# Six modulation sums move from VectorE to TensorE, and the weight ring becomes ten fixed blocks of 16 KB

## The chip, the cores and the metric

The kernel runs on one core of a Trainium2 chip. The metric is the device time of one execution in microseconds (us). A core has five instruction streams that matter here: TensorE (PE, the matrix engine, whose weight loads the profile lists apart as PEld), VectorE (DVE), ScalarE (ACT), GpSimd (POOL), and SyncE (SP), which issues all of this kernel's transfers (DMAs) between the main memory (HBM) and the on-chip memory (SBUF, 128 partitions). TensorE writes into PSUM, of which the kernel uses eight banks of 128x512 float32.

## The reference

One block of a network on 256 tokens of width 1024, all in float32: a modulated hybrid mixer and a mixture of experts.

```
mod = silu(c) @ w_ada + b_ada                    # [6 * 1024]
sh1, sc1, ga1, sh2, sc2, ga2 = split(mod, 6)
h = rms_norm(x, nw[0]) * (1 + sc1) + sh1
y = concat(gated_delta_rule(...), chunk_band_attention(...)) @ w_out    # both from h @ w_in
x = x + ga1 * rms_norm(y, nw[1])
h = rms_norm(x, nw[2]) * (1 + sc2) + sh2
top 4 of 32 experts per token from h @ w_router + b_router, softmax over the 4
expert e: hu = h @ w_up[e] + b_up[e]; glu = min(hu[:, :1024], 7); lin = clip(hu[:, 1024:], -7, 7)
          act = glu * sigmoid(1.702 * glu) * (lin + 1);  act @ w_down[e] + b_down[e]
x = x + ga2 * rms_norm(sum of gate * expert, nw[3])
```

The modulation is a product of one vector of 1024 with a matrix of 1024 x 6144, 25 MB. The experts' weights are 32 x 3 x 1024 x 1024 float32, 403 MB, and each of them is read once.

## The kernel before

**Stages.** The *front* computes the modulation, h, the projections, the delta rule (in the code `chain`), attention, the output projection, the second norm and the router. Then come the *experts*, in 14 groups.

**Modulation.** The matrix is cut into 12 chunks of 512 columns. A chunk in SBUF is a block of 128 x 8 x 512: row k * 128 + p of the matrix lies in partition p. Four chunks (sh1 and sc1) are summed first, by TensorE (`colvec`, L191). The eight others, the late chunks, are numbered 0 to 7: `seg` = i // 2 says which vector (0 ga1, 1 sh2, 2 sc2, 3 ga2) and `hf` = i % 2 which half of it. `ADA` (L28) gives the way in which each is summed, in `modrow` (L716):

- "D": VectorE multiplies row block 0 by silu(c) in place (L723) and adds the seven others with one multiply-add each (L725), 128x512 every one; then four matmuls against ones (L728) add over the partitions and put the sums into columns.
- "P": `colvec` does eight matmuls (L196) with silu(c), broadcast over 32 columns, as the stationary operand. Four of them at a time write four strips of 32 partitions of one bank. ScalarE copies the bank (L199), and four matmuls against an indicator (L201) add the strips and put the sums into columns.

After either, VectorE adds the bias and, where needed, the norm's weight (L733, L736). `ADATAG` says into which block a chunk is loaded (wF, or wB for chunks 2 and 7), so the chunks in wF follow one another: a chunk is loaded when the one before it has been read. `ADAPOS` says after which step of the projections, attention and output projection the chunk is written into the program (chunk 0 at 5, 4 at 8, 3 at 12, 6 at 19, 1 and 5 at 31; 2 at 6, 7 at 32).

**Order of work.** The program is written step by step, and then a planner orders each engine's instructions, SP's transfers too, by a simulated timeline, with the written order as priority; the `chain` is written with high priority. From L1043 to L1086 the order of TensorE and VectorE is as written: the second half of the output projection (`wout_a`), the residual, the second norm, the router.

**Splits.** The projections run as three products of rounded float32 (fp32r) pairs: `split` (L205) has ScalarE round a weight half-block of 128x2048 into a tile for the high part, and VectorE and GpSimd subtract it from the block to leave the low part there. The tiles for the high part come in turn from a pool tag "wh" with three buffers of 8 KB per partition; every third split uses the tag "h2" instead (`whx`). "h2", 8 KB, also holds, one after the other, x scaled (`xt`), attention's bias (`strip`) and the output projection's result (`yb`). After the 13 splits that use "wh" its turn stands at the second buffer.

**The ring.** The experts are ordered by load; a group holds 2 experts (P), 4 (Q) or 1 (S) side by side in the 128 rows of a matmul, in the order PQPPSQPPSQPPPP. For each of six weight blocks j (0 to 3 up, 4 and 5 down), a group loads one block of 2 MB per expert into the next places of a ring of ten (L23, `slot`, L1094). Eight places are fixed blocks of 16 KB per partition. The places "wh" and "wx" are made of two pool tiles of 8 KB each (`wslot`, L1098): wh of two buffers of the tag "wh", wx of the third and of "h2". `eload` (L1107) loads the blocks of one j in pieces: two in groups 0 (j = 5 only), 1 and 2, four for the last j of all, and otherwise one, but two for every block of that j when a place of it has two tiles:

```
tss = [wslot(slot()) for _ in regs]
m = 8 // max(pieces, max(len(ts) for ts in tss))
for k in range(0, 8, m):
    for reg, ts in zip(regs, tss):
```

Experts 0 and 1 of the order are loaded without waiting for the router. `group` (L1125) then runs, for each j, the 8 matmuls per expert (L1123, 512 columns), the activation, four transposes per half, and the products with the gates (L1172), which VectorE adds to the result.

Of the kernel before, what the change touches and what calls it, by code (L numbers as in the profile page):

```python
# [8 lines left out]
F32 = mybir.dt.float32  # L9
F32R = mybir.dt.float32r  # L10
# [9 lines left out]
NEG = -1e30  # L20
D = 1024
NE = 32
RINGTAGS = ["wB", "w0", "wC", "wE", "w1", "wD", "wF", "wh", "wA", "wx"]  # L23
PB = {"mm": 3, "dl": 3, "tp": 2}
K2 = 4
K1 = 6
KV = 2
ADA = list("DDPDDPDD")  # L28
ADATAG = list("FFBFFFFB")
ADAPOS = [5, 31, 6, 12, 8, 31, 19, 32]  # L30
ADABANK = "tp"
# [4 lines left out]

SINGLES, QUADS = 2, 3
ORDER = "PQPPSQPPSQPPPP"
WH = 3
RS_N = -2.0 * (-2.0 * (-2.0) ** 3) ** 3  # L40

C_C, C_BADA, C_NORM, C_CONV, C_AB, C_RT = 0, 8, 56, 88, 136, 200
# [7 lines left out]
def block_kernel(ctx, tc, x, small, rows, rel_ext, wpre, wexp, b_up, b_down, out,  # L50
                 dbg=None, stop=None):
    nc = tc.nc
    P = 128
# [5 lines left out]

    base = (nc.sbuf_base + 31) // 32 * 32
    ctx.enter_context(nc.sbuf_tensor("fixed", [P, 8 * 4096], F32))
    fixed = {}
    for i, tag in enumerate(("w0", "w1", "wA", "wB", "wC", "wD", "wE", "wF")):
        fixed[tag] = [nc.alloc_sbuf_tensor_at(f"{tag}_{d_}", (P, 4096), dt, offset=base + 16384 * i).ap()
                      for d_, dt in (("f", F32), ("r", F32R))]

    const = ctx.enter_context(tc.tile_pool(name="const", bufs=1))
    mem = ctx.enter_context(tc.tile_pool(name="mem", bufs=1))  # L70
    ps = ctx.enter_context(tc.tile_pool(name="ps", bufs=1, space=PSUM))

    def bank(tag="mm"):
        return ps.tile([P, 512], F32, tag=tag, bufs=PB[tag], name=tag)

    def block(tag):
        return fixed[tag][0]

    def wload(i, tag):
        t = block(tag)  # L80
        nc.sync.dma_start(t, wpre[i])
        return t.rearrange("p (k n) -> p k n", k=8)
# [86 lines left out]
        V.scalar_tensor_tensor(k2("junk"), srcs[1], 1.0, srcs[1], op0=ALU.mult, op1=ALU.mult, accum_out=pt_[:, 1:2])  # L169
        return pt_  # L170

    xt = mem.tile([P, 2, D], F32, tag="h2", name="xt")
    csil = const.tile([P, 8], F32, name="csil")
    rs1 = [rs_of(sumsq(f"ss1{a}", [x2[:, a, n * 512:n * 512 + 512] for n in range(2)]), D, f"rs1{a}", True)
           for a in range(2)]
# [24 lines left out]
        for m in range(4):  # L200
            T.matmul(out_cols[:, m:m + 1], ev[:, m * 128:(m + 1) * 128], ind, start=True, stop=True)  # L201

    nsp = [0]

    def split(w, kv=None, steps=1, extra=None, copy=None):  # L205


        sr, wl = w
        kv = kv or KV
        wh = extra  # L210
        if wh is None:
            wh = mem.tile([P, 2048], F32, tag="wh", bufs=WH, name="wh").bitcast(F32R)
        kn = sr.shape[1]
        wh = wh.rearrange("p (k n) -> p k n", k=kn)
        st = kn // steps
        for k in range(0, kn, st):
            (copy or S.copy)(wh[:, k:k + st], sr[:, k:k + st])
            m = k + kv // steps
            V.tensor_sub(wl[:, k:m], sr[:, k:m], wh[:, k:m])
            w_ = max(1, 512 // sr.shape[2])  # L220
            for i in range(m, k + st, w_):
                G.tensor_sub(wl[:, i:i + w_], sr[:, i:i + w_], wh[:, i:i + w_])
        return wh, wl
# [113 lines left out]
    V.tensor_copy(wabx[0], sm[:, C_AB:C_AB + 64])  # L337
    V.tensor_sub(wabx[1], sm[:, C_AB:C_AB + 64], wabx[0])
    kqT = mem.tile([P, 4, 2, 256], F32, tag="acc", name="kqT")
    whx = mem.tile([P, 2048], F32R, tag="h2", name="whx")  # L340
    spr = bank("dl")
    ws["q"] = hload(5, "wC")
    ws["qb"] = hload(6, "w0")
# [139 lines left out]
    yb = None  # L483
# [232 lines left out]
    def modrow(seg, hf, w):  # L716

        if ADA[2 * seg + hf] == "P":
            b_ = bank("tp")
# [23 lines left out]
        S.copy(dst[:, hf * 512:hf * 512 + 512], rb)  # L743

    def attention(blS):
        strip = mem.tile([P, 8, 256], F32, tag="h2", name="strip")
        nc.sync.dma_start(strip, bass.AP(tensor=rel_ext.tensor, offset=rel_ext.offset,
                                         ap=[[1, P], [384, 8], [1, 256]]))
        G.tensor_scalar(strip[0:64, :, 0:64], strip[0:64, :, 0:64], NEG, None, op0=ALU.add)
        jobs = [(0, 0), (1, 0), (1, 1)]  # L750
        st = {}

        def scores(a, gi):
            nk = 128 * (a + 1)
            hp = 512 // nk
            bs = [bank(), bank()]
            for i in range(hp):
                for par in range(2):
                    r_ = slice(64 * par, 64 * par + 64)
                    pr_ = gi * hp + i  # L760
                    T.matmul(bs[par][:, i * nk:(i + 1) * nk], qbT[r_, pr_, a * 128:(a + 1) * 128], kbT[r_, pr_, 0:nk],
                             start=True, stop=True)
            for par in range(2):
                h0 = 2 * gi * hp + par
                sc = blS[:, 512 * (2 * (a + gi) + par):512 * (2 * (a + gi) + par) + 512].rearrange("p (h k) -> p h k", h=hp)
                V.tensor_add(sc, bs[par].rearrange("p (h k) -> p h k", h=hp),
                             strip[:, h0:h0 + 2 * hp - 1:2, 0:nk][:, :, ::-1])
                mxs = const.tile([P, hp], F32, tag="mxs", bufs=3, name="mxs")
                V.tensor_reduce(mxs, sc, axis=AX.X, op=ALU.max, negate=True)
                dn = const.tile([P, hp], F32, tag="dens", bufs=3, name="dens")  # L770
                for i in range(hp):
                    S.activation(sc[:, i, :], sc[:, i, :], AF.Exp, bias=mxs[:, i:i + 1], accum_out=dn[:, i:i + 1])
                V.reciprocal(dn, dn)
                G.tensor_mul(sc, sc, dn[:, :, None].to_broadcast([P, hp, nk]))
                st[a, gi, par] = sc

        def trans(a, gi):
            nk = 128 * (a + 1)
            hp = 512 // nk
            for par in range(2):  # L780
                sc = st[a, gi, par]
                tp = bank("tp")
                for z_ in range(4):
                    i, kt = z_ // (a + 1), z_ % (a + 1)
                    T.transpose(tp[:, z_ * 128:(z_ + 1) * 128], sc[:, i, kt * 128:(kt + 1) * 128], ident)
                S.copy(sc.rearrange("p h (k t) -> p (h k t)", t=128), tp)

        def av(a, gi):
            nk = 128 * (a + 1)
            hp = 512 // nk  # L790
            if gi == 0:
                st["av", a] = bank()
            b_ = st["av", a]
            for i in range(hp):
                for kt in range(a + 1):
                    for par in range(2):
                        sc = st[a, gi, par].rearrange("p h (k t) -> p h k t", t=128)
                        pr_ = gi * hp + i
                        hd = 2 * pr_ + par
                        T.matmul(b_[64 * par:64 * par + 64, pr_ * 128:(pr_ + 1) * 128], vb[:, kt, hd * 64:(hd + 1) * 64],  # L800
                                 sc[:, i, kt, :], start=kt == 0, stop=kt == a)
            if gi == (0, 1)[a]:
                dst = oxb[0][:, :, a * 128:(a + 1) * 128]
                bv = b_.rearrange("p (k t) -> p k t", k=4)
                S.copy(dst, bv)
                V.tensor_sub(oxb[1][:, :, a * 128:(a + 1) * 128], bv, dst)

        for f, *at in ((scores, 0, 0), (scores, 1, 0), (trans, 0, 0), (scores, 1, 1), (av, 0, 0), (trans, 1, 0), (av, 1, 0),
                       (trans, 1, 1), (av, 1, 1)):
            f(*at)  # L810
            yield
# [48 lines left out]
        run(st_)  # L860

    pos = steps(mixed(), 17)
    yb = mem.tile([P, 2, D], F32, tag="h2", name="yb")
    wo.append(hload(19, "w1", 4))
    steps(wout_b(), pos)
    spa = [split(blk["wo"][n], kv=KW, extra=(fixed["w0"][1][:, 0:2048] if n == 0 else None)) for n in range(2)]
# [227 lines left out]
    def slot():  # L1094
        rtag[0] += 1
        return RINGTAGS[(rtag[0] - 1) % len(RINGTAGS)]

    def wslot(tag):  # L1098

        if tag in ("wh", "wx"):  # L1100
            ts = [mem.tile([P, 2048], F32, tag="wh", bufs=WH, name="wh") if tag == "wh" or i == 0 else
                  mem.tile([P, 2048], F32, tag="h2", name="wx") for i in range(2)]
        else:
            ts = [block(tag)]
        return [t.rearrange("p (k n) -> p k n", n=512) for t in ts]

    def eload(regs, j, pieces=1):  # L1107

        tss = [wslot(slot()) for _ in regs]
        m = 8 // max(pieces, max(len(ts) for ts in tss))  # L1110
        for k in range(0, 8, m):
            for reg, ts in zip(regs, tss):
                src = wexp[reg * 6 + j] if isinstance(reg, int) else wexp[bass.ds(reg * 6 + j, 1)].rearrange("o p n -> p (o n)")
                kt = 8 // len(ts)
                nc.sync.dma_start(ts[k // kt][:, k % kt:k % kt + m].rearrange("p k n -> p (k n)"), src[:, k * 512:(k + m) * 512])
        return [lambda k, ts=ts: ts[k * len(ts) // 8][:, k % (8 // len(ts)), :] for ts in tss]

    def expert_mm(b_, lhs, ws, last=True):

# [151 lines left out]

    fin = fixed[RINGTAGS[-4]][0].rearrange("p (i a d) -> p i a d", i=2, a=2)
    ss3 = const.tile([P, 4], F32, name="ss3")
# [7 lines left out]
    for gi, grp in enumerate(groups):  # L1281
        regs = [r if r < 2 else nc.sync.value_load(sig[0:1, r:r + 1], min_val=0, max_val=NE - 1) for r in grp]
# [26 lines left out]
    with tc.For_i(0, n_ov):  # L1309
# [14 lines left out]
        reg = nc.sync.value_load(eo[0:1, 0:1], min_val=0, max_val=NE - 1)  # L1324
# [77 lines left out]
```

## Time and profile before

| | us |
|---|---|
| median of 3 runs | 1191.61 |
| lowest and highest | 1190.53, 1195.18 |
| profiled execution, its own time | 1192.22 |
| its span, first to last instruction | 1190.4 |
| TensorE busy | 1029.8 (87%) |
| VectorE busy | 358.7 (30%) |
| ScalarE, GpSimd busy | 190.3 (16%), 104.1 (9%) |
| read from HBM | 449.50 MB, 379 GB/s over the span |

The profile is of one execution. "Busy" is the time in which an engine executes; idle time in brackets stands ahead of an instruction, with what ended it. Matmuls overlap, so a group's time is the union of its records. A float32 matmul leaves two records. The clock column is TensorE's granted clock, as a share of full speed. The names w_f and w_r stand for w0 and w1 together. "x16" is the number of instructions merged into one row; a row has its start, its time, engine, line, operation, and output <- input with shapes. For SP a row is an issue of a transfer, not its run.

### The profile page before, as it was taken

What the parts mean: (1) busy time and instruction counts of PE and PEld (TensorE: products, weight loads), DVE (VectorE), ACT (ScalarE), POOL (GpSimd) and SP (SyncE); (2) the same over time, 40 slices, a digit from 0 to 9 for tenths busy, and PEclk for the clock granted to TensorE, in tenths of its full rate; (3) what the DMA queues carried; (4) which work ended last, traced back from release to release, by engine and by line L of the source; (5) the groups of instructions that cost most, each with busy time, mean ns of one, the idle gap of its engine ahead of it and who ended that gap; (6) DMA issues with size and microseconds to landing.
All of it is one profiled execution on the core that took longest, in us unless ns stands there. A gap on an engine that the chain in (4) does not pass through costs nothing. (4 is left out here: it accounts for less than half of the span.)

```text
span 1190.4 us, 14727 instructions
## 1 busy us (share of the span) xinstructions
PE 1029.8 (87%) x5845; PEld 495.3 (42%) x5845; DVE 358.7 (30%) x851; ACT 190.3 (16%) x380; POOL 104.1 (9%) x91
## 2 busy tenths in 40 slices
PE   4898999899977789999976788989967698998985
PEld 2697998654321224435421233335322142433331
DVE  5387888654103022122111012122201011111113
ACT  3453327331001001011000001011001001010101
POOL 1557514200000000000000000000000000000001
PEclk9899999989998999999997999999988899999998
DMA  9925346989999999999999999999999999999993
GB/s 362 403 81 213 142 178 237 401 353 386 421 421 422 421 408 426 423 428 423 423 422 424 427 425 426 424 427 425 420 426 425 423 427 423 426 426 422 428 419 149
DMA packets 51463, 451.93 MB, mean 380 GB/s; under 512 B 5760, under 2 KB 7424, under 8 KB 9408
## 3 DMA queue, kind: packets, MB, share of 16 engines
q1 hardware_dynamic: 51392, 450.97, 91.3%
q8 instruction: 47, 0.77, 0.3%
q14 instruction: 24, 0.20, 0.0%
HBM read 449.50 MB, written 1.05 MB: 379 GB/s over the span
## 5 line engine op out<-in xcount | busy, mean ns | idle before, releaser
L1123 PE MATMUL dl<-w_f,xg 128*64 128x512 f32 (+1 forms) x224 | 113.5, 653 | 9.7 <-DMA w_f<-in_wexp_dram 9.7
L1177 DVE TENSOR_TENSOR acc<-acc,mm 128x512 f32<-128x512 f32 x52 | 35.8, 688 | 242.2 <-PE mm L1172 242.2
L1123 PE MATMUL mm<-w_f,xg 128*64 128x512 f32 (+2 forms) x208 | 92.7, 594 | 4.0 <-DMA w_f<-in_wexp_dram 4.0
L1279 POOL TENSOR_TENSOR wF_f<-acc,m_row 128x512 f32<-128x512 f32 x3 | 3.8, 1273 | 943.1 <-DMA w_f<-in_wexp_dram 937.3
L1123 PE MATMUL dl<-wh,xg 128*64 128x512 f32 (+2 forms) x144 | 70.3, 633 | 5.1 <-DMA wh<-in_wexp_dram 5.1
L1123 PE MATMUL dl<-wD_f,xg 128*64 128x512 f32 (+1 forms) x128 | 65.4, 662 | 4.3 <-DMA wD_f<-in_wexp_dram 4.3
L1172 PE MATMUL mm<-yg,wts 128*128 128x512 f32 x112 | 54.5, 614 | 11.0 <-ACT yg L1169 10.0
L1141 ACT ACTIVATE sg<-gm 128x512 f32<-128x512 f32 x28 | 17.6, 630 | 288.9 <-DVE gm L1139 263.1
L1123 PE MATMUL dl<-wE_f,xg 128*64 128x512 f32 (+2 forms) x112 | 55.2, 645 | 6.4 <-DMA wE_f<-in_wexp_dram 6.4
L1123 PE MATMUL mm<-wB_f,xg 128*64 128x512 f32 (+2 forms) x128 | 57.6, 595 | 0.0
L1123 PE MATMUL mm<-wh,xg 128*64 128x512 f32 (+1 forms) x144 | 57.1, 594 | 0.5 <-DMA wh<-in_wexp_dram 0.5
L1123 PE MATMUL dl<-wF_f,xg 128*64 128x512 f32 (+2 forms) x112 | 54.5, 628 | 2.8 <-DMA wF_f<-in_wexp_dram 2.8
L1123 PE MATMUL dl<-wC_f,xg 128*64 128x512 f32 (+2 forms) x112 | 55.4, 638 | 1.4 <-DMA wC_f<-in_wexp_dram 1.4
L1003 PEld LDWEIGHTS tp<-oh,x 128*128 128x128 f32 x432 | 50.7, 192 | 13.2 <-issue 11.4
L1003 PE MATMUL tp<-oh,x 128*128 128x128 f32 x432 | 54.8, 279 | 0.7 <-ACT aT__3377 L1152 0.7
L1123 PE MATMUL mm<-wE_f,xg 128*64 128x512 f32 (+1 forms) x112 | 49.6, 595 | 3.9 <-DMA wE_f<-in_wexp_dram 3.9
L1169 ACT COPY yg<-dl 128x512 f32<-128x512 f32 x27 | 15.8, 585 | 224.8 <-PE dl L1123 224.8
L1123 PE MATMUL dl<-wB_f,xg 128*32 128x512 f32 (+1 forms) x96 | 47.7, 634 | 3.5 <-DMA wB_f<-in_wexp_dram 3.5
L1013 DVE TENSOR_SCALAR xg<-tp,mc,mc 128x128 f32<-128x128 f32 x52 | 19.6, 405 | 101.1 <-PE dl L1123 92.4
L1123 PE MATMUL mm<-wC_f,xg 128*64 128x512 f32 (+1 forms) x112 | 50.0, 594 | 0.0
L1123 PEld LDWEIGHTS dl<-w_f,xg 128*64 128x64 f32 (+1 forms) x224 | 28.2, 134 | 42.6 <-issue 25.7
L1139 DVE TENSOR_SCALAR gm<-dl 128x512 f32<-128x512 f32 x14 | 9.7, 692 | 119.5 <-PE dl L1134 119.5
(640 smaller groups left out, 2193.3 us busy)
## 6 DMA issues: line engine op xcount, KB each, us to landing
wh<-in_wexp_dram SPq DMA_DIRECT2D x57, 1024.0 KB, 24.7
w_f<-in_wexp_dram SPq DMA_DIRECT2D x26, 2048.0 KB, 26.1
wA_f<-in_wexp_dram SPq DMA_DIRECT2D x36, 1024.0 KB, 22.2
wF_f<-in_wexp_dram SPq DMA_DIRECT2D x36, 1024.0 KB, 29.7
wE_f<-in_wexp_dram SPq DMA_DIRECT2D x15, 2048.0 KB, 29.4
wC_f<-in_wexp_dram SPq DMA_DIRECT2D x15, 2048.0 KB, 27.0
wB_f<-in_wexp_dram SPq DMA_DIRECT2D x13, 2048.0 KB, 22.2
wD_f<-in_wexp_dram SPq DMA_DIRECT2D x13, 2048.0 KB, 34.2
```

Of the source, the lines that this page charges most:

```text
L1003: T.matmul(b_[:, k * 128:(k + 1) * 128], x2[:, a, half(n)][:, k * 128:(k + 1) * 128], oh[:, a], start=a == tiles[0], stop=a == tiles[-1])
L1013: V.tensor_scalar(xg[:, k], src, mc, sc, op0=ALU.mult, op1=ALU.add)
L1123: T.matmul(b_[i * n:(i + 1) * n, :], lhs[:, k, i * n:(i + 1) * n], w(k), start=k == 0, stop=last and k == 7)
L1139: V.tensor_scalar(gm, bs[0], 7.0, None, op0=ALU.min)
L1141: S.activation(sg, gm, AF.Sigmoid, scale=1.702)
L1169: S.copy(yg, b_)
L1172: T.matmul(cb, wt[:, a], yg, start=True, stop=True)
L1177: V.tensor_add(acc[:, a, sl], acc[:, a, sl], cb)
L1279: (V if a and n else G).tensor_mul(fin[:, 0, a, sl], acc[:, a, sl], m3_row[:, sl])
```

## The change

All eight late chunks are summed in the form "P". The fixed region grows from eight to ten blocks of 16 KB: wG and wH are new. The high parts of the splits now lie, in turn, in the first half of wG, the second half of wG and the first half of wH (`highs`), and what used the tag "h2" lies in the second half of wH (`h2`). The pool tags "wh" and "h2" go, so the memory in use stays the same. In the ring wG and wH stand where wh and wx stood, and `eload` no longer cuts their sets in two.

```diff
-RINGTAGS = ["wB", "w0", "wC", "wE", "w1", "wD", "wF", "wh", "wA", "wx"]
+RINGTAGS = ["wB", "w0", "wC", "wE", "w1", "wD", "wF", "wG", "wA", "wH"]
...
-ADA = list("DDPDDPDD")
+ADA = list("PPPPPPPP")
...
-    ctx.enter_context(nc.sbuf_tensor("fixed", [P, 8 * 4096], F32))
+    ctx.enter_context(nc.sbuf_tensor("fixed", [P, 10 * 4096], F32))
...
+    highs = [fixed["wG"][1][:, 0:2048], fixed["wG"][1][:, 2048:4096], fixed["wH"][1][:, 0:2048]]
+    nsp = [0]
+
+    def h2(dt=0):
+        return fixed["wH"][dt][:, 2048:4096]
...
-    xt = mem.tile([P, 2, D], F32, tag="h2", name="xt")
+    xt = h2().rearrange("p (a n) -> p a n", a=2)
...
-            wh = mem.tile([P, 2048], F32, tag="wh", bufs=WH, name="wh").bitcast(F32R)
+            wh = highs[nsp[0] % 3]
+            nsp[0] += 1
...
-    whx = mem.tile([P, 2048], F32R, tag="h2", name="whx")
+    whx = h2(1)
...
-        strip = mem.tile([P, 8, 256], F32, tag="h2", name="strip")
+        strip = h2().rearrange("p (h k) -> p h k", h=8)
...
-    yb = mem.tile([P, 2, D], F32, tag="h2", name="yb")
+    yb = h2().rearrange("p (a n) -> p a n", a=2)
...
     def eload(regs, j, pieces=1):
 
-        tss = [wslot(slot()) for _ in regs]
-        m = 8 // max(pieces, max(len(ts) for ts in tss))
+        ts = [block(slot()).rearrange("p (k n) -> p k n", n=512) for _ in regs]
+        m = 8 // pieces
         for k in range(0, 8, m):
...
```

## Rows read from the trace of the kernel before

**Rows 1.** Busy us by stage: PE, PEld, DVE, ACT, POOL; then granted clock, DMA share, GB/s.

```profile
100.00:120.00 20.00, 15.77 (x159) 13.72 (x159) 17.96 (x18) 6.86 (x9) 16.94 (x11) 0.88 0.50 195
...
140.00:160.00 20.00, 20.00 (x247) 19.22 (x246) 18.43 (x30) 4.20 (x9) 4.49 (x3) 1.00 0.59 219
...
260.00:270.00 10.00, 10.00 (x52) 3.44 (x53) 1.47 (x3) 2.75 (x4) 0.00 (x0) 1.00 0.78 284
...
330.00:412.00 82.00, 61.00 (x329) 18.36 (x331) 14.14 (x46) 4.79 (x10) 0.00 (x0) 0.94 1.01 421
...
470.00:496.00 26.00, 24.54 (x124) 10.48 (x124) 4.14 (x6) 1.80 (x3) 0.00 (x0) 1.00 1.00 426
...
1160.00:1170.00 10.00, 9.33 (x39) 3.15 (x36) 0.29 (x2) 1.17 (x2) 0.00 (x0) 1.00 0.85 338
```

**Rows 2.** VectorE's multiply-adds, as a group (60 to 222 us), then by time.

```profile
L725 DVE SCALAR_TENSOR_TENSOR wF_f<-wF_f,csil 128x512 f32<-128x512 f32 x35 | 34.9, 997 | 0.7
...
113.04 2.71 DVE L725 SCALAR_TENSOR_TENSOR wF_f<-wF_f,csil 128x512 f32<-128x512 f32 x1
...
115.67 1.39 DVE L621 TENSOR_TENSOR wE_f<-id,dl 64x512 f32<-64x512 f32 x2
```

**Rows 3.** TensorE by time: the matmuls of colvec (start, us, line, operation).

```profile
215.19 1.92 PE L196 MATMUL tp<-wF_f,csil 128*32 128x512 f32 x16
```

**Rows 4.** TensorE by time after it; idle time and what ended it in brackets.

```profile
217.82 1.05 PE L201 MATMUL tp<-ind,ev 128*128 128x1 f32 x8 [0.71 <-ACT ev L199]
...
221.26 1.12 PE L891 MATMUL tp<-ident,wE_f 128*128 128x128 f32 x4 [1.49 <-DVE mc L733]
```

**Rows 5.** TensorE by time, around 116 us and at full clock.

```profile
116.39 2.69 PE L595 MATMUL dl<-wE_f,Lm 64*64 64x64 f32 x32 [3.73 <-DVE wE_f L621]
...
119.82 1.91 PE L232 MATMUL mm<-wD_r,wA_r 128*128 128x256 f32 x8
...
127.28 1.12 PE L232 MATMUL mm<-wD_r,wA_r 128*128 128x256 f32 x8
...
154.00 1.15 PE L595 MATMUL dl<-wE_f,Lm 64*64 64x64 f32 x32
```

**Rows 6.** SP's DMA issues by time, in the stream of the experts.

```profile
478.23 0.33 SPq L1115 DMA_DIRECT2D wh<-in_wexp_dram  x1
...
497.80 0.33 SPq L1115 DMA_DIRECT2D wx<-in_wexp_dram  x1
...
500.28 0.33 SPq L1115 DMA_DIRECT2D wB_f<-in_wexp_dram  x1
...
515.20 0.33 SPq L1115 DMA_DIRECT2D wF_f<-in_wexp_dram  x1
```

**Rows 7.** SP's DMA issues by time, the first fill of the ring.

```profile
211.72 3.03 SPq L1115 DMA_DIRECT2D wh<-in_wexp_dram  x2
...
215.29 0.33 SPq L1115 DMA_DIRECT2D w_f<-in_wexp_dram  x1
...
235.09 0.33 SPq L1115 DMA_DIRECT2D wh<-in_wexp_dram  x1
...
243.28 0.33 SPq L1115 DMA_DIRECT2D wx<-in_wexp_dram  x1
...
261.05 0.33 SPq L1115 DMA_DIRECT2D wB_f<-in_wexp_dram  x1
```

**Rows 8.** TensorE by time, in the last group.

```profile
1142.54 1.10 PE L1123 MATMUL dl<-wD_f,xg 128*64 128x512 f32 x1 [0.24 <-DMA wD_f<-in_wexp_dram]
...
1150.52 0.59 PE L1123 MATMUL dl<-wF_f,xg 128*64 128x512 f32 x1
...
1157.61 0.59 PE L1123 MATMUL dl<-wA_f,aT__6140 128*64 128x512 f32 x1
...
1163.32 0.64 PE L1123 MATMUL dl<-wA_f,aT__6140 128*64 128x512 f32 x1 [0.67 <-ACT aT__6140 L1152]
```

**Rows 9.** DMA issues by transfer: count, KB each, median us to landing.

```profile
wF_f<-in_wpre_dram SPq DMA_DIRECT2D x6, 2048.0 KB, 8.0
```

More of the change, by code (lines that the diff above doesn't have):

```diff
@@ L38 @@
 ORDER = "PQPPSQPPSQPPPP"
-WH = 3
 RS_N = -2.0 * (-2.0 * (-2.0) ** 3) ** 3
@@ L62, in block_kernel @@
     base = (nc.sbuf_base + 31) // 32 * 32
-    ctx.enter_context(nc.sbuf_tensor("fixed", [P, 8 * 4096], F32))
+    ctx.enter_context(nc.sbuf_tensor("fixed", [P, 10 * 4096], F32))
     fixed = {}
-    for i, tag in enumerate(("w0", "w1", "wA", "wB", "wC", "wD", "wE", "wF")):
+    for i, tag in enumerate(("w0", "w1", "wA", "wB", "wC", "wD", "wE", "wF", "wG", "wH")):
         fixed[tag] = [nc.alloc_sbuf_tensor_at(f"{tag}_{d_}", (P, 4096), dt, offset=base + 16384 * i).ap()
@@ L201, in colvec @@
             T.matmul(out_cols[:, m:m + 1], ev[:, m * 128:(m + 1) * 128], ind, start=True, stop=True)
-    nsp = [0]
     def split(w, kv=None, steps=1, extra=None, copy=None):
@@ L1096, in slot @@
         return RINGTAGS[(rtag[0] - 1) % len(RINGTAGS)]
[L1098 to L1105, printed above, removed]
     def eload(regs, j, pieces=1):
-        tss = [wslot(slot()) for _ in regs]
-        m = 8 // max(pieces, max(len(ts) for ts in tss))
+        ts = [block(slot()).rearrange("p (k n) -> p k n", n=512) for _ in regs]
+        m = 8 // pieces
         for k in range(0, 8, m):
-            for reg, ts in zip(regs, tss):
+            for reg, t in zip(regs, ts):
                 src = wexp[reg * 6 + j] if isinstance(reg, int) else wexp[bass.ds(reg * 6 + j, 1)].rearrange("o p n -> p (o n)")
-                kt = 8 // len(ts)
-                nc.sync.dma_start(ts[k // kt][:, k % kt:k % kt + m].rearrange("p k n -> p (k n)"), src[:, k * 512:(k + m) * 512])
-        return [lambda k, ts=ts: ts[k * len(ts) // 8][:, k % (8 // len(ts)), :] for ts in tss]
+                nc.sync.dma_start(t[:, k:k + m].rearrange("p k n -> p (k n)"), src[:, k * 512:(k + m) * 512])
+        return [lambda k, t=t: t[:, k, :] for t in ts]
     def expert_mm(b_, lhs, ws, last=True):
```

## The prediction

> **What bounds the kernel now.** I read the busy table by stages first. It has three regimes. Up to about 245 us the modulation, the projections, the delta rule, attention and the output projection run (the front). Here TensorE is the full engine: 20.00 us busy of 20 at 140 to 160, and 15.77 of 20 at 100 to 120, with VectorE at 18.43 and 17.96 beside it, while the transfers use only half of their time (shares 0.59 and 0.50) [rows 1]. From 260 us TensorE is full and the transfers are not (0.78 at 260 to 270, with TensorE 10.00 of 10): the ring of ten places is loaded, and a place is filled again only after TensorE has read it. Soon after, the transfers are full (1.01 over 330 to 412, 1.00 over 470 to 496) and stay so until near the end: over 1160 to 1170 their share is 0.85, so the last byte has landed at about 1168.5 [rows 1]. So the time is: the end of the front, plus a stream of expert weights at its own rate, plus what TensorE still owes when the stream is over. The reader should see three places where a microsecond counts in full: TensorE's queue in the front, the rate of the stream, and the last group.
>
> The profiled execution took 1192.22 us with a span of 1190.4, so 1.8 us lie around it; it is 0.6 us above the median of the runs, 1191.61. Sums below are made against 1192.22.
>
> **Part 1, six chunks go from VectorE to TensorE.** Chunks 2 and 5 were TensorE's already; 0, 1, 3, 4, 6 and 7 change. Each loses one multiplication and seven multiply-adds on VectorE: 35 multiply-adds in wF take 34.9 us, 997 ns each [rows 2]; seven more in wB and the six multiplications come on top, over 40 us in all. Each gains eight matmuls of colvec, 16 records since each float32 matmul is two. Such a group takes 1.92 us in the trace, start of the first to end of the last, its four column strips side by side [rows 3]; there is one more like it. The four matmuls behind it that bring the sums into columns (1.05 us) [rows 4] stand where the old form had four of the same shape, so they cost nothing. So TensorE's queue grows by 6 x 1.92 = 11.5 us, and ScalarE gets six copies of 128x512, for which it has room (6.86 busy of 20 at 100 to 120) [rows 1]. The matmul behind such a copy waits for it: 0.71 us in the trace [rows 4], 0 to 4.3 us for six; I take 0, since other matmuls can stand between, and keep 4.3 for the bound.
>
> What comes back: where VectorE holds up TensorE. At 116.39 us TensorE has been idle 3.73 us for a VectorE subtraction at 115.67, which stands behind one multiply-add of chunk work that took 2.71 us [rows 2, 5]. Its clock fell with the pause (granted 0.88 over these 20 us, so partly at 1.2 instead of 2.4 GHz): the 32 records that follow take 2.69 us against 1.15 at 154.00, and the next eight-record group 1.91 against 1.12 for the same shape at 127.28 [rows 5], about 2.3 us. With the chunk gone from VectorE that is 3.7 + 2.3 = 6.0 us. At 217.82 and 221.26 TensorE waits another 0.71 and 1.49 us, the second time for a modulation column that VectorE wrote late [rows 4]; these 2.2 us I count as regained too. Next in line after that is TensorE's own work, so no more comes back. Between full cover (the 11.5 vanish and 8.2 come back, -8.2) and none (+11.5 + 4.3 = +15.8) I take 11.5 - 8.2 = +3.3, because the stretches at 100% leave nothing to hide the columns in.
>
> **Part 2, the places.** Before, wh took two tiles of a pool of three and wx the third and h2, and whenever one of them was in a set of loads all of that set went in halves of 1 MB. Now they go whole, but for the groups 0 to 2 and the last j, which keep their pieces. Counting by slots (12, 24, 12, 12, 6, 24, 12, 12, 6, 24, 12, 12, 12, 12 over ten places), in groups 3 to 13 there are 6+4+4+4+6+6+4 = 34 such slots in pairs, 2 in singles and 16+12 = 28 in quads: 64 slots of 2 MB change. In the stream SP's issues wait for the landing of earlier ring transfers, eight back by the names, so their distance is the landing distance: (497.80 - 478.23)/4 = 4.893 us per whole slot, (515.20 - 500.28)/6 = 2.487 per half, 4.973 per slot [rows 6]. 64 x 0.080 = 5.1 us less. The rates over longer stretches bound it from the other side: 421 GB/s with halves only, 426 with whole slots [rows 1], so 4.981 against 4.923 us, 64 x 0.058 = 3.7. I take the 5.1, since the issues separate the sizes cleanly; the bounds are 0 and 5.1.
>
> The first fill: wh could be loaded at 211.72, when the first half of the output projection was done, and only half of wx waited until 235.09 and 243.28 [rows 7]. By the fixed addresses wG holds the high part of the last split, which the output projection reads to the end, so its 2 MB start at about 235 and all of wH at 243. On SP's queue only wC, wD and wH stand behind that wait, which are free no sooner (wC and wD hold operands of the same projection). The nine slots that remain at 215.29 flow at some 4.95 us each, so the fill ends at 215.29 + 9 x 4.95 = 259.8, before the first place is refilled at 261.05 [rows 7]. Price 0; if the front got shorter without the transfers, up to 4 us.
>
> The tail: in the last group wF with wh and wA with wx came in halves, so TensorE could begin on the first half. At 1142.54 it begins j = 2 just as wD lands; j = 3 begins at 1150.52 and j = 4 at 1157.61 [rows 8]. Landing whole, 4.9 us apart after 1142.5, the pair of j = 3 is there at 1152.3 and that of j = 4 at 1162.1. j = 3 takes 7.1 us and ends at 1159.4, so j = 4 starts at 1162.1, 4.5 us late; of that the pause before 1163.32 (transposes and their copy, 1.3 us) is passed in the new wait. About +3.0 us, from 0 (if TensorE lags behind the stream) to 7 (two more pauses, after each of which some four steps run 0.5 us longer, as after the one before 1142.54: 1.10 us against 0.59 at 1150.52).
>
> Sum: 1192.2 + 3.3 - 5.1 + 3.0 = 1193.4; less the 0.6 to the median, 1192.8, told as 1193.
>
> **Rivals.** *VectorE sets the pace of the front.* Then the chain of the delta rule gets shorter as over 40 us of chunk work leave VectorE, the columns fall into gaps, and the front ends 4 us sooner: 1191.6 - 4 - 5.1 + 1.5 = 1184 (half the price of the tail, as TensorE then starts the ring earlier). For it: 18.43 of 20 on VectorE, the stretched instructions. Against: TensorE has no gaps at 140 to 160. *The front is TensorE's alone, and the order written anew regains nothing.* The pauses were an accident of that order; they reappear elsewhere, with six waits for copies: 1191.6 + 15.8 - 5.1 + 3.0 = 1205.3. It decides, that is slower by over 6 us, from the point where the front grows by more than 8.1 us (8.1 - 5.1 + 3.0 = 6). For it: 100% busy; against: the 3.73 us behind chunk work. *The size of a transfer does not matter to the rate*: 1192.8 + 5.1 = 1197.9, slower but at the edge. *Each DMA pays for its start alone*: a lone 2 MB load lands 8.0 us after its issue [rows 9], 3.1 more than its 4.9 in the stream; if each paid that, 64 fewer would save 198 us, 1192.8 + 5.1 - 198 = 1000. Against it: neighbours of 1 MB land 2.487 us apart [rows 6]. The Trainium skill, "DMA: Bandwidth & Descriptors", section "Anatomy of one DMA — SWDGE (gpsimd) path", fits about 2.0 us fixed to each DMA on another descriptor path; 64 fewer would save 128 us by it if they did not overlap, and the trace disagrees, since in a queue they do.
>
> **Chances.** Forecast 0.51, VectorE's pace 0.25, TensorE's order 0.20, no effect of size 0.03, start cost 0.01. A measurement of this kernel can't tell less than about 0.5% (6 us) from no change. The forecast's own range is 1187 to 1197. Faster 0.26, same 0.52, slower 0.22 (part of the size case lies there). To hold 8 in 10 the range takes in most of both rivals: 1183 to 1204.
>
> **What would show it.** TensorE: eight times 1.92 us of colvec and no pause behind VectorE near 110 to 120. First refill at 264 instead of 261 us. From then on 4.89 us per slot and 428 GB/s. In the last group pauses ahead of j = 3 and j = 4, and more time from the end of the stream to the end. I am wrong if the first refill moves by more than 6 us either way, or if the stream does not speed up.

## The result, and the profile after

The changed kernel takes 1204.88 us (median of 4 runs, 1202.61 to 1207.41) against 1191.61: ratio 1.0111, 95% interval 1.0095 to 1.0126. It is slower by 13.3 us and lies 0.9 us outside the predicted range; the prediction was wrong. The profiled execution took 1202.61 us with a span of 1200.8, 10.4 us more than that of before, so the trace accounts for 10.4 of the 13.3 us. Ratios here and below leave out three single executions that took far longer (2953.14 us of the kernel before, 5636.71 of the run named places, 1718.85 of the run named tail).

The time splits at two points that the prediction named: the first refill of the ring, which ends the front, and the last byte of the stream. The issues of SP in the kernel after (start, us, line, operation, transfer):

```profile
228.13 0.33 SPq L1110 DMA_DIRECT2D wF_f<-in_wexp_dram  x1
...
247.65 0.33 SPq L1110 DMA_DIRECT2D wG_f<-in_wexp_dram  x1
...
255.97 0.33 SPq L1110 DMA_DIRECT2D wH_f<-in_wexp_dram  x1
...
273.25 0.33 SPq L1110 DMA_DIRECT2D wB_f<-in_wexp_dram  x1
...
1165.43 0.33 SPq L1110 DMA_DIRECT2D wB_f<-in_wexp_dram  x1
1170.32 0.33 SPq L1110 DMA_DIRECT2D w_f<-in_wexp_dram  x1
```

The refill comes at 273.25 where it came at 261.05 [rows 7]: the front grew by 12.2 us. The stages of the kernel after, with the columns of [rows 1]:

```profile
100.00:120.00 20.00, 20.00 (x168) 16.86 (x168) 6.54 (x12) 9.54 (x12) 14.22 (x10) 1.00 0.57 224
...
470.00:496.00 26.00, 25.29 (x110) 9.79 (x108) 4.14 (x6) 2.35 (x4) 0.00 (x0) 1.00 1.01 428
1160.00:1170.00 10.00, 7.96 (x38) 2.87 (x38) 2.08 (x3) 0.50 (x2) 0.00 (x0) 1.00 0.99 412
1170.00:1180.00 10.00, 9.76 (x45) 3.35 (x46) 0.00 (x0) 1.13 (x2) 0.00 (x0) 1.00 0.74 298
```

VectorE is relieved (6.54 us busy for 17.96 at 100 to 120), and TensorE has neither a pause nor a fall of the clock there. Reckoned by the transfers' share, as in the prediction, the stream ends at 1170 + 0.74 x 10 = 1177.4, so it lasts 904.2 us, 3.3 less than the 1168.5 - 261.05 = 907.5 of before; from there to the end of the span are 23.4 us for 21.9. The sum is 12.2 - 3.3 + 1.5 = 10.4. So the loss is made in the front, after 120 us. The stages of before (first fence) and after (second), with TensorE alone (busy us, granted clock, DMA share, GB/s):

```profile
180.00:200.00 20.00, 19.07 (x174) 1.00 0.77 308
```

```profile
180.00:200.00 20.00, 19.07 (x167) 0.53 0.33 122
```

Busy alone shows nothing: 19.07 both times. The clock column does: over these 20 us TensorE ran at about half speed, 20 x (1 - 0.53) = 9.4 us of work at 2.4 GHz not done. In windows of 2 us it begins here (columns as in [rows 1]):

```profile
176.00:178.00 2.00, 1.04 (x16) 1.00 (x16) 1.94 (x4) 1.55 (x5) 0.01 (x1) 1.00 1.02 426
178.00:180.00 2.00, 2.00 (x12) 1.64 (x11) 1.80 (x4) 2.00 (x4) 1.04 (x1) 0.56 1.11 471
180.00:182.00 2.00, 2.00 (x24) 2.00 (x24) 1.78 (x3) 0.47 (x3) 0.34 (x1) 0.50 0.95 406
...
196.00:198.00 2.00, 2.00 (x11) 2.00 (x11) 0.42 (x1) 0.38 (x1) 0.00 (x0) 0.50 0.59 115
198.00:200.00 2.00, 2.00 (x17) 2.00 (x16) 0.13 (x1) 0.37 (x1) 0.00 (x0) 0.82 0.71 279
```

What stood in TensorE's queue at that time (by time; idle time and its end in brackets):

```profile
173.35 2.53 PE L600 MATMUL dl<-wB_f 64*64 64x64 f32 x48
176.96 1.14 PE L600 MATMUL dl<-wB_f 64*64 64x64 f32 x16 [1.08 <-DVE wE_f L638]
...
190.33 1.97 PE L667 MATMUL dl<-wB_f 64*64 64x64 f32 x16 [0.47 <-ACT wB_f L658]
192.76 2.08 PE L689 MATMUL dl<-wE_f 128*128 128x128 f32 x8 [0.47 <-ACT wE_f L658]
194.63 1.91 PE L693 MATMUL dl<-wE_f,wB_f 128*128 128x128 f32 x8
...
199.26 1.06 PE L705 MATMUL dl<-wE_f 128*128 128x128 f32 x8
...
203.51 0.69 PE L714 MATMUL dl<-vn,wE_f 128*128 128x128 f32 x4
```

This is the end of the delta rule's chain, and nothing else: from 173.35 to 202.56 no scores, projections or attention stand between its levels. The same form takes 1.06 us at full clock (at 199.26) and 2.08 here (at 192.76). The chain begins later in the new order, so the projections are used up before its last levels come. Its first level in the kernel after:

```profile
130.58 1.15 PE L600 MATMUL dl<-id,Lm 64*64 64x64 f32 x32
```

In the kernel before the first level ran at 108.24, and other work, as here the product of L800, lay between the later steps:

```profile
108.24 1.15 PE L595 MATMUL dl<-id,Lm 64*64 64x64 f32 x32 [0.49 <-DVE Lm L588]
...
188.25 1.06 PE L684 MATMUL dl<-wE_f 128*128 128x128 f32 x8
189.24 1.09 PE L800 MATMUL mm<-w_f,wC_f 128*64 128x128 f32 x14
...
202.71 1.05 PE L709 MATMUL dl<-vn,wE_f 128*128 128x128 f32 x8
```

The chain itself ends when it did, at 203.8 us before and 204.2 after. What changed is the work of attention and the output projection that now stands behind it. One more row group, the new columns over 60 to 249.2 us by form, where before had one of each form with 1.9 us:

```profile
L202 PE MATMUL tp<-wF_f,csil 128*32 128x512 f32 x96 | 14.7, 599 | 0.9 <-DMA wF_f<-in_wpre_dram 0.9
...
L202 PE MATMUL tp<-wB_f,csil 128*32 128x512 f32 x32 | 3.8, 598 | 0.0
```

That is 18.5 us for eight columns; less the 3.8 of the two of before, 14.7 for six, 2.45 each and not 1.92. Three of the six are cut in two by other work, as here:

```profile
152.99 1.90 PE L202 MATMUL tp<-wF_f,csil 128*32 128x512 f32 x10
...
156.83 1.06 PE L202 MATMUL tp<-wF_f,csil 128*32 128x512 f32 x6
```

The four strips lie side by side only inside a piece, so 10 and 6 records cost 1.90 + 1.06 where 16 together cost 1.92.

The theory to be tested: the sums, not the places, make the front late; their own work is most of it, and the half clock of the chain's lone end gives back what the pause at 116 had cost. Rivals: the addresses of the places do it; the clock is of no account, since the chain waits for its copies anyway; the columns' work does not count, only the lone stretch.

### The profile page after: what moved, and what is told of

Read it like the earlier page. It is cut to its first block, busy times and chain, and to the rows that moved or that the text cites. A ratio compares the mean times of both kernels' runs of the same rounds, so it can differ in the third digit from the quotient of the medians.

```text
span 1200.8 us, 14656 instructions
## 1 busy us (share of the span) xinstructions
PE 1043.3 (87%) x5941; PEld 498.1 (41%) x5941; DVE 315.3 (26%) x803; ACT 193.3 (16%) x386; POOL 100.5 (8%) x91
## 5 line engine op out<-in xcount | busy, mean ns | idle before, releaser
L1167 PE MATMUL mm<-yg,wts 128*128 128x512 f32 x112 | 54.5, 614 | 12.3 <-ACT yg L1164 11.3
L1118 PE MATMUL dl<-wG_f,xg 128*64 128x512 f32 (+2 forms) x112 | 54.6, 636 | 8.1 <-DMA wG_f<-in_wexp_dram 8.1
L1118 PE MATMUL dl<-wE_f,xg 128*64 128x512 f32 (+2 forms) x112 | 52.3, 615 | 3.4 <-DMA wE_f<-in_wexp_dram 3.4
L1164 ACT COPY yg<-dl 128x512 f32<-128x512 f32 x27 | 15.8, 585 | 235.2 <-PE dl L1118 235.2
L1016 ACT ACTIVATE xg<-tp,mc,mc 128x128 f32<-128x128 f32 x52 | 21.8, 454 | 129.2 <-DVE xg L1018 129.2
L1118 PE MATMUL mm<-wH_f,xg 128*64 128x512 f32 (+1 forms) x96 | 42.5, 594 | 0.1
```

The costliest lines, as they stand in the source:

```text
L1016: S.activation(xg[:, k], src, AF.Identity, scale=mc, bias=sc)
L1118: T.matmul(b_[i * n:(i + 1) * n, :], lhs[:, k, i * n:(i + 1) * n], w(k), start=k == 0, stop=last and k == 7)
L1164: S.copy(yg, b_)
L1167: T.matmul(cb, wt[:, a], yg, start=True, stop=True)
```

## The experiments

Ratios are to the kernel before, timed beside it on the same chip. Edits are against the changed kernel unless said otherwise.

**places: the fixed places alone.**

```diff
-ADA = list("PPPPPPPP")
+ADA = list("DDPDDPDD")
```

> The ten fixed places alone; chunks 0, 1, 3, 4, 6 and 7 stay with VectorE as before. Theory (the sums write TensorE's order anew, the last levels of the delta rule's chain then stand alone in its queue, and the granted clock there is 0.50): nothing of that happens here; first refill at about 261 us as before, granted clock 1.00 at 180 to 200, stream 3 us shorter (904 for 907 us), end 1.3 us longer: about 1190. Rival 'the addresses make the front late': refill at about 273 and clock 0.53 at 180 to 200, about 1203. Rival 'the colvecs simply add': as the theory here.

Measured: 1191.15 us, ratio 0.9997 (0.9982 to 1.0013). Its trace comes from one more execution of the same kernel:

> The fixed places alone once more, for its trace: first refill at 261, granted clock 1.00 over 180 to 200, stream some 3 us shorter than before, last group some 1.3 us longer; span about 1188 to 1190.

It took 1191.4 us, with a span of 1189.5. By TensorE's stages and SP's first refill:

```profile
100.00:120.00 20.00, 14.51 (x150) 0.91 0.29 107
...
180.00:200.00 20.00, 18.69 (x176) 1.00 0.77 315
...
412.00:1060.00 648.00, 567.28 (x2682) 0.95 1.01 426
```

```profile
261.82 0.33 SPq L1110 DMA_DIRECT2D wB_f<-in_wexp_dram  x1
```

No half clock at 180 to 200, the refill 0.8 us later than before, the pause at 116 still there (5.5 us idle in 100 to 120). The stream is at 426 GB/s for 424 in the kernel before:

```profile
412.00:1060.00 648.00, 565.70 (x2674) 215.77 (x2672) 112.32 (x229) 56.52 (x111) 0.00 (x0) 0.96 1.01 424
```

In sum the places are worth about nothing, and not the cause.

**sums: the eight sums alone, in the old places** (against the kernel before).

```diff
-ADA = list("DDPDDPDD")
+ADA = list("PPPPPPPP")
```

> All eight chunks summed by TensorE, the places as before. Theory: refill at 273 us, granted clock about 0.5 over some 20 us near 180 to 200, stream 907 us, end 22 us: 1192 + 12 = about 1204. Rival 'the addresses make the front late': no lone stretch, refill at 261 to 264, about 1192 to 1195. Rival 'the colvecs simply add' (6 x 1.92 = 11.5 us, nothing regained, the clock of no account): refill 272.5, also about 1204, but the pause of 3.73 us behind VectorE near 116 us still there.

Measured: 1205.14 us, 1.0118 (1.0100 to 1.0136); refill at 272.41; clock over 180 to 200 0.56; no pause at 116. The whole loss is in the sums, and the lone stretch comes in either layout.

**heat: extra work in the lone stretch.**

```diff
+        def extra(src):
+            T.matmul(bank("tp"), ident, src, start=True, stop=True)
...
             ub = pair_mm(Ti, X)
...
+            if s_ >= 4:
+                for _ in range(HEAT):
+                    extra(X.rearrange("p c n -> p (c n)"))
```

> The changed kernel with 13 extra float32 matmuls of 128x512 into a bank that nobody reads, from the fourth level of the chain to its end, each reading a tensor of the chain: about 0.45 us each at 2.4 GHz by the 112 of L1167 (54.5 us with overlap), so some 6 us more work. Theory (the clock of the lone stretch costs some 10 us): granted clock 1.00 over 178 to 200, the stretch loses 10 and gains 6, refill at about 269, time about 1201, 2 to 6 us below the changed kernel. Rival 'the clock is of no account, the chain waits for its copies': refill unchanged at 273 (the extra work lies in the waits), time as the changed kernel or up to 6 us above. Rival 'the colvecs simply add': 6 us more work is 6 us more time, refill 279, 1211.

Measured: 1209.08 us, 1.0140 (1.0118 to 1.0161). There were eleven of them, not thirteen, and they took 11.6 us in the trace, not 6 (the 112 of the expectation are records, two to a matmul). The clock over 180 to 200 was 1.00, and the refill came at 280.02, 6.8 us later for 11.6 us of work. A miss for the number: 4.8 us of the added work came at no cost, and whether the clock paid for them or waits that were there already, this run does not tell.

**warm: less of it**, seven matmuls of half the width.

```diff
+            T.matmul(bank("tp")[:, 0:256], ident, src[:, 0:256], start=True, stop=True)
```

> The changed kernel with seven extra float32 matmuls of 128x256 into a bank that nobody reads, over the last two levels and the end of the chain: about 0.5 us each (the 128x512 ones of the run named heat took 1.0), 3.5 us of work. Theory 'the clock of the lone stretch costs wall time': granted clock above 0.9 over 180 to 200, refill at 267 to 271. Rival 'TensorE's own work, the clock of no account': refill at 276 to 277. If the clock stays at 0.5 with these, nothing is told apart.

Measured: 1201.73 us, 1.0090 (1.0064 to 1.0117). The added work took 4.7 us. TensorE over 180 to 200, and the first refill:

```profile
180.00:200.00 20.00, 19.50 (x176) 1.00 0.45 160
```

```profile
269.70 0.33 SPq L1121 DMA_DIRECT2D wB_f<-in_wexp_dram  x1
```

The front is 3.55 us shorter with 4.7 us more work in it. The edit moved more than it says: the pause of 1.08 us ahead of 176.96 is gone, and the planner put one of the new columns, cut in three, among the chain's products (191.38 to 197.4). Since the interval overlaps that of the changed kernel, both were timed side by side on one chip:

> The changed kernel once more, beside the next two on one chip: refill near 273, granted clock about 0.53 over 180 to 200, 1203 to 1207.

> The kernel named warm once more, timed beside the changed kernel on one chip. Theory 'the half clock of the lone stretch costs 7 us of wall time, of which the 3.5 us of extra work give back 3.5': 3 to 4 us below after_b. Rival 'the lower trace of warm was chance': 3.5 us above it.

Measured: after_b 1204.49 us, 1.0108 (1.0095 to 1.0121); warm_b 1203.33 us, 1.0097 (1.0084 to 1.0110). The difference is -1.3 us, with an interval of about 2.2 either way: it may be nothing, the 3 to 4 of the theory lie at its edge, and the rival's +3.5 is out. If the 4.7 us of work would otherwise have counted in full, holding the clock is worth some 6 us (4.7 + 1.3), with the same 2.2 either way. The traced refills agree with no difference, 269.52 in warm_b and 268.67 in after_b. But the profiled execution of after_b, the same program in the same order, shows the price of the clock without any added work, since the clock came back sooner in it:

```profile
178.00:180.00 2.00, 2.00 (x13) 0.50 1.06 451
180.00:182.00 2.00, 2.00 (x30) 0.70 1.01 430
182.00:184.00 2.00, 2.00 (x40) 1.00 0.74 303
...
180.00:200.00 20.00, 18.38 (x206) 0.88 0.46 180
```

```profile
268.67 0.33 SPq L1110 DMA_DIRECT2D wB_f<-in_wexp_dram  x1
```

```profile
197.76 0.69 PE L714 MATMUL dl<-vn,wE_f 128*128 128x128 f32 x4
```

At 0.88 for 0.53 the chain's last matmuls start at 197.76 for 203.51, though both executions have the same pause of 1.08 us, 0.36 us apart (176.60 and 176.96): 5.4 us go with the clock of this stretch. The refill comes at 268.67 for 273.25, so 4.6 of them are left at the end of the front. The medians of the two runs agree (1204.49 and 1204.88); how often the clock comes back sooner is not shown.

**short: half of the new columns' work.**

```diff
-        for k in range(8):
+        for k in range(ks):
...
-            colvec(w, csil, b_, ADABANK)
+            colvec(w, csil, b_, ADABANK, 8 if 2 * seg + hf in (2, 5) else 4)
```

> The changed kernel with half of each of the six new columns' work: k = 0 to 3 alone in chunks 0, 1, 3, 4, 6 and 7 (the other half of their sums is left out), the same loads and the same copies. A group of eight takes 1.92 us, two records alone 1.04, so about 0.9 less each. Theory 'TensorE's own work': 6 x 0.9 = 5.4 us less on the front, refill at 267 to 268, about 1199. Rival 'the lone stretch at half clock decides': the columns ahead of the stretch do not matter, refill at 271 to 273, 1202 to 1205.

Measured: 1204.45 us, 1.0113 (1.0090 to 1.0137), as the changed kernel, though the traced execution had its refill at 269.63. In it a new pause of 2.84 us behind VectorE stands in the lone stretch, at clock 0.63. Taken alone it speaks for the rival, so it was repeated with the clock held:

> warm with the six new columns at half their work as in the run named short (the other half of their sums is left out). With the clock held, theory 'the columns' work counts in full': 5 to 6 us below warm_b, refill near 264, about 1196. Rival 'the columns' work does not count, only the lone stretch': as warm_b.

Measured: 1199.34 us, 1.0046 (1.0030 to 1.0063), against 1.0097 for warm_b: 6 us less (0.0051, with about 0.0021 either way, 2.5 us; the medians differ by 4.0). In the traces, both at clock 1.00 over 180 to 200, the eight columns take 13.4 us for 19.5, 6.1 less. The traced refill is at 268.20 for 269.52, not near 264; in this execution the clock was lower elsewhere (0.91 for 1.00 over 40 to 80, 0.74 for 0.83 over 240 to 260: 5.4 us). So with the clock of the stretch held the columns' work counts, and in full as far as this interval tells. Without that, work taken from the columns was lost again in the stretch.

**later and spread: orders that keep other work between the chain's levels.**

```diff
-ADAPOS = [5, 31, 6, 12, 8, 31, 19, 32]
+ADAPOS = [5, 31, 6, 25, 8, 31, 28, 32]
```

> The changed kernel with chunks 3 and 6 issued at places 25 and 28 of the steps for 12 and 19; all eight are still summed by TensorE, and the order written keeps scores, projections and attention between the last levels of the chain. Theory: granted clock above 0.85 over 178 to 200, no lone stretch, refill at 263 to 267, about 1193 to 1198. Rival 'the colvecs simply add': the same 11.5 us more on TensorE, refill at 273 or later, 1203 or more. Against both, later loads of two chunks through wF could make the output projection wait: then the clock is 1.00 and pauses behind DMA wF_f appear after 200 us.

```diff
-ADATAG = list("FFBFFFFB")
-ADAPOS = [5, 31, 6, 12, 8, 31, 19, 32]
+ADATAG = list("FBBFFFFB")
+ADAPOS = [5, 28, 6, 25, 8, 31, 28, 32]
```

> All eight chunks by TensorE, in an order that keeps scores, projections and attention between the last levels of the chain (chunks 1, 3 and 6 issued at steps 28, 25 and 28), and without the queue of four late loads through wF of the run named later: chunk 1 goes through wB, so three go through wF and two through wB. Theory (order and clock): granted clock 1.00 over 180 to 200, the chain ends near 193 as in that run, no wait of over 1.5 us behind DMA wF_f after it, first refill at 262 to 266, about 1193 to 1196. Rival 'the columns add up' (11.5 us whatever the order): refill at 273, 1203 or more.

Measured: later 1206.39 us, 1.0137 (1.0115 to 1.0158), refill 275.99; spread 1205.30 us, 1.0104 (1.0083 to 1.0124), refill 273.98. Half of the theory came true: clock 1.00 over 180 to 200, and the chain ends at 194 and 197 us for 204. The other half fell: the refill did not move. TensorE in spread, first by stages, then by time:

```profile
180.00:200.00 20.00, 18.99 (x164) 1.00 0.90 363
200.00:220.00 20.00, 12.42 (x96) 0.83 0.67 269
```

```profile
204.78 1.92 PE L202 MATMUL tp<-wB_f,csil 128*32 128x512 f32 x16 [1.64 <-DMA wB_f<-in_wpre_dram]
...
220.25 3.48 PE L202 MATMUL tp<-wF_f,csil 128*32 128x512 f32 x16 [4.57 <-DMA wF_f<-in_wpre_dram]
```

The chunks that come later wait for their loads, as the expectation of later had named for a third case, and behind the wait of 4.57 us the column takes 3.48 us for 1.92. In the traces of four kernels with all eight sums (changed, sums, later, spread) the front ends between 272.4 and 276.0; in after_b, where the clock came back sooner, at 268.67.

**two and less: one step each way** (with the fixed places). Two chunks more by TensorE, then one less:

```diff
-ADA = list("DDPDDPDD")
+ADA = list("PDPDPPDD")
```

> The fixed places, and chunks 0, 2 and 4 by TensorE (before: 2 and 5): chunk 4 is the one whose multiply-add stood before the 3.73 us pause at 116. Theory: the pause and its half clock go (7.6 us of idle and lost clock at 100 to 120 in the trace of before), chunks 0 and 4 come (2 x 1.92 = 3.8) and chunk 5 goes (1.9, but late, behind a load), and the order keeps the filler between the chain's levels: refill at 255 to 260, about 1185 to 1190. Rival 'every colvec adds 1.92 and nothing comes back': refill at 263, 1193 or more.

```diff
-ADA = list("DDPDDPDD")
+ADA = list("DDDDDPDD")
```

> The fixed places, and chunk 2 too goes back to VectorE (only chunk 5 is left to TensorE): the change the other way. Theory now ('TensorE's own work sets the front, and the pauses come back elsewhere whatever the order'): one colvec less, some 2 to 2.5 us, refill at 259 to 260 for 261.8, about 1189. Rival 'VectorE holds up TensorE': the pause behind VectorE near 116 grows past 4.35 us or a second one comes, refill at 264 or more, 1194.

Measured: two 1194.53 us, 1.0016 (1.0003 to 1.0030), refill 264.92. (Its expectation counts wrongly: chunk 5 stays with TensorE, so two columns are added and none goes.) The pause at 116 is gone, and still the front got no shorter, where 255 to 260 was expected. That two columns cost time is not clear of noise: the time is 0.0019 above places, with about 0.0021 either way, and the refill of places2, halves, tail and tail2, whose late chunks are summed as in places, lies anywhere from 260.04 to 264.25. Less: 1198.59 us, 1.0049 (1.0033 to 1.0066), refill 269.48. Here VectorE does hold up TensorE:

```profile
75.11 3.78 PE L237 MATMUL mm<-wA_r,wH_r 128*128 128x256 f32 x16 [3.98 <-DVE cacc L360]
...
119.96 3.47 PE L600 MATMUL dl<-wB_f 64*64 64x64 f32 x46 [3.48 <-DVE wB_f L632]
```

So the old assignment stands between: one chunk less on TensorE costs VectorE's pauses, two more gain nothing.

**halves: the price of 1 MB transfers** (against places).

```diff
-PIECES.get(gi, 1) if gi
+PIECES.get(gi, 2 if gi < len(groups) - 1 else 1) if gi
```

> The fixed places with the old chunks, and every slot of groups 3 to 12 loaded in two halves of 1 MB in place of 2 MB whole: 12+6+24+12+12+6+24+12+12+12 = 132 slots. By 0.080 us per slot from the distances of the issues: 10.6 us longer; by 0.058 from the rates, 7.7; by the 3.1 us that 64 slots gave in the stream of the changed kernel, 0.048 each, 6.4. Rival 'the size of a transfer does not matter': 0, as the places alone, 1191.

Measured: 1202.83 us, 1.0092 (1.0075 to 1.0109); against places 0.0095, 11.3 us for 132 slots, 0.086 each, with about 0.02 either way. The stretch of the row above for places2, in halves:

```profile
412.00:1060.00 648.00, 573.11 (x2666) 0.97 1.01 420
```

The price from the distances of the issues (0.080) lies within this, and size matters.

**tail and tail2: the two cheap gains put together** (against places). Both load j = 3 and j = 4 of the last group in two pieces again; tail loads group 2 whole, tail2 groups 1 and 2.

```diff
-PIECES = {0: 2, 1: 2, 2: 2}
+PIECES = {0: 2}
...
+2 if gi == len(groups) - 1 and j in (3, 4) else
```

> The fixed places with the old chunks, group 2 loaded whole for in halves (12 slots less in halves, at 0.086 us each by the run named halves, 11.4 us for 132), and j = 3 and j = 4 of the last group in two pieces again, the rest whole. By the price of the halves: 1.0 us less in the stream, and the 1.3 us that the end lost with whole slots come back: 1188 to 1190, ratio to before 0.996 to 0.999. Rival: TensorE in group 2 waits for whole slots and the ring gets later: 1192 or more.

> The kernel named tail with group 1 loaded whole as well (24 slots less in halves, 0.086 us each by the run named halves: 2.1 us): 1187 to 1189, ratio to before 0.995 to 0.998. Rival: the second group follows the first so closely that TensorE waits for whole slots at about 280 to 300 us, and nothing is gained: 1190 to 1192.

Measured: tail 1190.36 us, 0.9977 (0.9962 to 0.9991); tail2 1186.83 us, 0.9957 (0.9940 to 0.9974). The stretch that was at 421 GB/s in the kernel before [rows 1] is at 428 in tail2 (over the same 300 to 412 us both kernels have 421):

```profile
300.00:412.00 112.00, 83.53 (x506) 0.88 1.01 428
```

tail2 beats both kernels: 5 us under the kernel before (3 to 7 by its interval), with the fixed places and the old sums.

## Why the prediction was wrong

**Where the time lies** was read rightly: TensorE's queue in the front, the rate of the stream, the last group. The three moved by +12.2, -3.3 and +1.5, where +3.3, -5.1 and +3.0 were predicted.

**The step that failed** is the sum of part 1: "I take 11.5 - 8.2 = +3.3", with the reason "the stretches at 100% leave nothing to hide the columns in" and "no more comes back". Both terms were looked at alone, and the order around them was taken to stay.

- The columns: 6 x 1.92 = 11.5 was mis-sized. They took 14.7, as three were cut in two.
- What comes back was right in size: the pause at 116 and its half clock did go. Over 100 to 140 us the trace of before has 4.6 us of pauses and 3.4 us of lost clock (the length of a stretch times what its granted clock lacks to 1.00), the changed one none. That is 8.0 us where the prediction had 6.0 there and 8.2 in all; its other 2.2, the small waits at 218 and 221, return elsewhere (0.94 us behind wF at 226, 0.71 behind a copy at 234).
- What the step left out: the new order lost as much again. 9.4 us of clock went in the lone end of the chain. Against 14.7 + 9.4 - 8.0 = 16.1 the traced front grew by 12.2. The other 3.9 lie at 20 to 80 us, where pauses and lost clock came to 17.2 us before and 13.2 after. There the granted clock differs between executions: over 20 to 40 it was 0.83 in the trace of the changed kernel and 0.91 in after_b, the same program.

Added up over the whole front, from 20 us to the refill, TensorE's pauses and lost clock were 20.5 + 19.0 = 39.5 us before and 19.1 + 16.9 = 36.0 after; the rest, its own work, is 201.6 and 217.2 us. So the work grew by 15.6 us, about what the six columns take, and of pauses and lost clock only 3.5 us came back on balance, no more than the 3.9 of 20 to 80 us.

That the lone stretch costs wall time is shown by the two traces of the changed kernel (some 5 us, where over 180 to 200 us one lost 9.4 us of clock and the other 2.4); warm_b fits it, with the added work taken at full price. That the columns' work is the greater part is shown by this sum and fits shortwarm. What stays open: why the order written begins the chain 22 us later. VectorE has written the input of its first level at 106.3 us, as before (105.9). Its next step of the chain (L593) stands behind steps of a column and of splits that wait for other engines:

```profile
105.61 0.69 DVE L585 TENSOR_TENSOR wB_f<-wE_f 64x512 f32<-64x512 f32 x1
...
115.12 0.16 DVE L738 SCALAR_TENSOR_TENSOR mc<-tp,sm 128x4 f32<-128x4 f32 x1 [8.52 <-PE tp L207]
...
126.53 2.37 DVE L593 TENSOR_TENSOR Lm<-wB_f,lvm 128x512 f32<-128x512 f32 x2
```

Why the planner set them in this order no run tells.

The Trainium skill, "TensorE: Matmul & The Clock Gate", section "Part 1: The HAM clock gate (the "warmup" mystery)", lets the clock depend on how busy TensorE has just been. The trace agrees where the clock falls, at 178 behind 2 us with 1.04 us busy. It does not agree that a busy engine gets it back, if busy is read from the records: they show 2.00 of 2 us at 180 to 182 and 196 to 198, and the clock stays at 0.50.

**The rival that won** is "the front is TensorE's alone, and the order written anew regains nothing", chance 0.20, 1205.3 us against 1204.88 measured. So close a hit is in part luck: its front, stream and tail were +15.8, -5.1 and +3.0, and the trace has +12.2, -3.3 and +1.5. Its statement held in all four kernels with eight sums: what was regained was lost elsewhere. Its mechanism (six waits for the copies, 4.3 us) did not: that was 0.7 us, and the clock of the lone stretch or late loads took the rest. "VectorE sets the pace" is refuted by the result itself and by two: VectorE was relieved, and the front got no shorter. Less shows that the other direction has the pauses.

**The places.** The stream: -5.1 predicted, -3.3 measured. The price per slot fits halves (0.080, and 0.086 with 0.02 either way), so why 64 slots gave less than 5.1 us stays open. The size of a transfer does matter, and the start of each is not paid alone in a queue: the last issues of the stream, quarters that each wait for a whole slot of earlier loads to land, lie 1170.32 - 1165.43 = 4.89 us apart. The first fill: price 0, as foreseen (in places2 the refill is at 261.82). In the changed kernel the fill ends behind the refill, since wH, issued at 255.97, lands 20.2 us later; no wait of TensorE for a transfer shows from 262 to 345 us. The tail: +3.0 predicted, +1.5 measured, with the pause ahead of j = 3 as foreseen and a shorter one ahead of j = 4:

```profile
1160.46 0.64 PE L1118 MATMUL dl<-wG_f,xg 128*64 128x512 f32 x1 [1.44 <-DMA wG_f<-in_wexp_dram]
...
1170.24 0.64 PE L1118 MATMUL dl<-wH_f,aT__6009 128*64 128x512 f32 x1 [0.32 <-DMA wH_f<-in_wexp_dram]
```

## What to carry to other kernels

Where an order is planned from costs, work that moves from one engine to another writes the order of all of them anew: price the moved work and then ask which dependent chain loses the work that lay between its steps. A pause that goes is no gain until the next one is known, and the next one need not look like a pause: read the granted clock beside the busy time, for a queue that is 95% busy can run at half speed. Between one engine with pauses and another that is full, try one step each way before moving everything.

## What had not been expected of the hardware

- TensorE stayed at 1.2 GHz for some 20 us (178 to 198) with 64x64 and 128x128 float32 matmuls almost back to back in its records, after one pause of 1.08 us. In warm, with seven matmuls of 128x256 among them and without that pause, it kept 2.4 GHz.
- The same program got the clock back after some 3 us in one execution (and lost it for some 3 more at 188) and after some 20 in another, with 4.6 us between the two refills.
- Eight matmuls in four strips of 32 columns cost 1.92 us together and 2.96 when cut into 10 and 6 records.
- In a full queue, 1 MB transfers move 420 GB/s where 2 MB ones move 426 to 428.
